# An encoder layer's output projection: where the squares for its RMS norm are added up, and on which engine

## The chip, the cores and the metric

The kernel runs on one core of a Trainium2 chip. The metric is the device time of one execution in microseconds (us); lower is better. Before the change the median of three runs is 1039.83 us, from 1038.88 to 1041.15.

## The reference

One encoder layer over 1024 tokens of width 1024. Two groups of attention heads (a sliding window and a two-dimensional neighbourhood) share one input projection; their outputs, each with an RMS norm of its own, go through one output projection. A gated MLP with a short convolution follows, and a last RMS norm:

```python
mix = jnp.concatenate([rmsnorm(o_a, norm_a[l]), rmsnorm(o_b, norm_b[l])], axis=-1)
h = h + jnp.einsum('bse,ed->bsd', mix, w_out[l])
hn = rmsnorm(h, norm_ffn[l])
h = h + conv_gated_mlp(hn, w_gate[l], w_up[l], conv_w[l], conv_b[l], w_down[l])
```

The norm divides each token by the root of the mean of its 1024 squares plus 1e-6. The change is in how `rmsnorm(h, norm_ffn[l])` gets its sums of squares, and in the first weights of the MLP.

## The kernel before, in words

Features lie on partitions: `h1[d]` (d = 0 to 7) holds 128 features of all 1024 tokens, and `at(d, h)` is its half h of 512 tokens. Products run in pairs of high and low float16 parts, three matmuls for one, accumulated in PSUM.

**The order of work.** TensorE's order is the order of the program text (`manual_schedule` for that engine). The order on the other engines is set by a planner, which takes what its estimates say is ready, by the order of the program, and earlier for what stands under `tc.high_priority(offset=...)`. Each engine then works strictly in the order that it was given, so an instruction that waits holds up all behind it on its engine.

**The output projection's second part** (group B's four input tiles) is the loop over half h and tile d. Each (h, d) is one product of twelve matmuls (L180, `product16`, which yields after each three), written to the PSUM banks `o`, `s` and `pj` in turn. `settle_out` follows it: VectorE adds the product onto `h1` (L1199), ScalarE's queue sends `h1` to DRAM (L1200), and ScalarE squares it into a tile `s2` (L1203). For d = 1, 2 and 3 VectorE adds the square onto the running total (L1205). From d = 3 on, the total and the four squares after it are addends, five a half: `sum_up` (L1216) sums each over its partitions with four matmuls whose moving operand is one column of `ones` (1/1024), into four columns of a PSUM bank, 128 tokens each. It does so two products later, so that TensorE need not wait. `inverse_root` adds EPS on VectorE (L1221) and raises to the power -0.5 on GpSimd (L1222). `widen` (L263) spreads the result over 128 partitions with four transposes, into the PSUM bank `sw`, and `normed` (L1227) multiplies `h1` by it. `operands` (L1183 on ScalarE, L1184 on VectorE) makes the float16 pairs `hg`: `B[1, 1]` from d = 0 to 3 and `B[2, 1]` from d = 4 to 7 of half 0.

**The MLP** uses a Strassen-like scheme of seven products a weight block, `p1` to `p7`, with sums of blocks of weights and of operands. The first four blocks (`HEAD`) are prepared inside the projection's loop: `settle_scales` finds scales, `pure` and `two_parts` (L1067, L1068) split weights, `head_weights` (L1237 for "s1", L1229 for later sums and differences) adds blocks of weights, and `split_w` (L1150, L1151) splits them. `units[0].p1()`, `units[1].p1()`, `units[0].p2()` and `units[1].p2()` follow the projection at once; the `p1` read `B[1, 1]` and the `p2` read `B[2, 1]`. Half 0's `widen` stands after product (1, 2), half 1's after `units[1].p2()`. Half 1's operands `B["t1"]` and on come from it.

**Buffers.** The squares and the four weight sums `wsum` share eight buffers of the tag `tt`; the weight sums keep four of them.

**A helper that is there already** (L221 to L225), and that the change calls. It sums over partitions by transposing into a bank and reducing:

```python
def inverse_power(sq, dim, tag):
    ps = bank("st", tag)
    for c in range(4):
        nc.tensor.transpose(ps[:, c * 128:(c + 1) * 128], sq[:, c * 128:(c + 1) * 128], ident)
    v = cpool.tile([128, 4], F32, name="v4", tag="v4", bufs=4)
    nc.vector.tensor_reduce(v, ps[:, :].rearrange("p (c w) -> p c w", w=128), axis=mybir.AxisListType.X, op=ALU.add)
    nc.vector.tensor_scalar(v, v, 1.0 / dim, EPS, op0=ALU.mult, op1=ALU.add)
    nc.gpsimd.tensor_tensor(v, v, minus_half, op=ALU.pow)
    return v
```

Of the kernel before, what the change touches and what calls it, by code (L numbers as in the profile page):

```python
# [13 lines left out]
F32 = mybir.dt.float32  # L14
# [4 lines left out]
ALU = mybir.AluOpType  # L19
PSUM = bass.MemoryType.PSUM  # L20

D, S, HD = 1024, 1024, 64
KT = D // 128
# [6 lines left out]
EPS = 1e-6  # L30
# [33 lines left out]
def hybrid_layer(tc, xT, w_in, w_out, w_gate, w_up, w_down, small, sink, rpb, consts, rope, out):  # L64
    nc = tc.nc
    with ExitStack() as ctx:
        pool = lambda name, bufs, **kw: ctx.enter_context(tc.tile_pool(name=name, bufs=bufs, **kw))
        cpool = pool("const", 1)
# [12 lines left out]
        def big(name, tag, dt=F32):  # L81
            return lpool.tile([128, S], dt, name=name, tag=tag, bufs=slots[tag])
# [9 lines left out]
        def bank(name, tag):  # L92
            return psum.tile([128, HALF], F32, name=name, tag=tag)
# [7 lines left out]
        ones = cpool.tile([128, 128], F32, name="ones")  # L101
# [5 lines left out]
        minus_half = cpool.tile([128, 4], F32, name="minus_half")  # L107
# [68 lines left out]
        def product16(ps, ws, xs, h):  # L176

            for i, (w, x) in enumerate(zip(ws, xs, strict=True)):
                for a, b in ((w[0], x[h][0]), (w[0], x[h][1]), (w[1], x[h][0])):
                    nc.tensor.matmul(ps, a, b, start=i == 0 and b is x[h][0] and a is w[0], stop=i == len(ws) - 1 and a is w[1])  # L180
                yield
# [35 lines left out]
# [10 lines that stand above are left out]
# [393 lines left out]
        mg, h1, norm = [None] * 8, [None] * KT, {}  # L620
# [106 lines left out]
        t = quarters(big("f", "mix"))  # L727
# [174 lines left out]
        for g in range(2):  # L902
            for b in range(NB):
                q, t, w = unit_window(g, b)
# [52 lines left out]
        for u in range(len(flat)):  # L957
            q, t, need, kind, _ = flat[u]
# [105 lines left out]
        def two_parts(view, src, by):  # L1064

            hi, lo = view
            nc.scalar.activation(hi, src, AF.Copy, scale=by)  # L1067
            nc.vector.scalar_tensor_tensor(lo, src, by, hi, op0=ALU.mult, op1=ALU.subtract)  # L1068
            return [(hi[:, j, :], lo[:, j, :]) for j in range(4)]

        def parts_places():

            t = big("wp", "op").bitcast(F16)[:, :].rearrange("p (d s k c) -> p d s k c", d=2, s=2, c=128)
            return [(t[:, i, 0], t[:, i, 1]) for i in range(2)]

        def pure(f):
            raw, by = head_raw[f][0], scale_of[f]
            to = parts_places()
            W[f, "11"], W[f, "12"] = two_parts(to[0], raw[:, 0:4], by), two_parts(to[1], raw[:, 4:8], by)
# [8 lines left out]
        def load_wo(d, pools):  # L1088
            raw = wo_raw.pop(d)
            if d % 2 == 0:  # L1090
                wo_raw["t"] = big("wo", "op").bitcast(F16)[:, :].rearrange("p (d s j c) -> p d s j c", d=2, s=2, c=128)
            t = wo_raw["t"][:, d % 2]
            with tc.high_priority(offset=300):
                nc.scalar.activation(t[:, 0], raw, AF.Copy, scale=wo_by)
                with behind(*["rows"] * (d >= 2)):
                    nc.vector.scalar_tensor_tensor(t[:, 1], raw, wo_by, t[:, 0], op0=ALU.mult, op1=ALU.subtract)
            return [(t[:, 0, j, :], t[:, 1, j, :]) for j in range(4)]
# [6 lines left out]
        with behind("flip", "xr"):  # L1104
            for d in range(0, WO_EARLY, 2):
                t = big("wr", "op")[:, :].rearrange("p (d j c) -> p d j c", d=2, c=128)
# [9 lines left out]
        for h in range(2):  # L1116
# [9 lines left out]
            if h == 0:  # L1126
                wo = [load_wo(d, wpool) for d in range(2)]
# [62 lines left out]

        K1, K2 = range(0, 4), range(4, 8)
        B = {}
        late, total, addends, narrow, ADDED = [], [None, None], [], [None, None], (4, 4)
        at = lambda k, h: h1[k][:, tsl(h)]

        def settle_out():
            d, h, ps = late.pop(0)
            with tc.high_priority(offset=300):
                nc.vector.scalar_tensor_tensor(at(d, h), ps, wo_back, at(d, h), op0=ALU.mult, op1=ALU.add)  # L1199
            nc.scalar.dma_start(spilled[d][:, tsl(h)], at(d, h))  # L1200
            s2 = half("s2")
            with tc.high_priority(offset=300):
                nc.scalar.activation(s2, at(d, h), AF.Square)  # L1203
                if 0 < d < ADDED[h]:
                    nc.vector.tensor_tensor(s2, s2, total[h], op=ALU.add)  # L1205
            total[h] = s2
            if d >= ADDED[h] - 1:
                addends.append((h, d, s2))

        def sum_up(until=2 * KT):  # L1210
            while addends and KT * addends[0][0] + addends[0][1] <= until:
                h, d, s2 = addends.pop(0)
                if d == ADDED[h] - 1:
                    narrow[h] = bank("ss", "pt")
                for c in range(4):
                    nc.tensor.matmul(narrow[h][:, c:c + 1], s2[:, c * 128:(c + 1) * 128], ones[:, 0:1], start=c == 0 and d == ADDED[h] - 1,  # L1216
                                     stop=d == KT - 1, skip_group_check=True)

        def inverse_root(h):
            v = cpool.tile([128, 4], F32, name="v4", tag="v4", bufs=4)  # L1220
            nc.vector.tensor_scalar(v, narrow[h][:, 0:4], EPS, None, op0=ALU.add)  # L1221
            nc.gpsimd.tensor_tensor(v, v, minus_half, op=ALU.pow)  # L1222
            return v

        def normed(h, wide, ds):
            for d in ds:
# [6 lines left out]
        def head_weights(i, name):  # L1233
            f, t = FO[i], wsum[i]
            g, u = head_raw[f]
            if name == "s1":
                nc.vector.tensor_tensor(t, u[:, 0:4], u[:, 4:8], op=ALU.add)  # L1237
            elif name == "s2":
                sub(t, t, g[:, 0:4])
            elif name == "s4":  # L1240
                sub(t, g[:, 4:8], t)
            elif name == "s3":
                sub(t, g[:, 0:4], u[:, 0:4])
            else:
                t = u[:, 4:8]
            if name == "s1":
                if i % 2 == 0:
                    s1_places.extend(parts_places())
                W[f, name] = two_parts(s1_places.pop(0), t, scale_of[f])
            else:  # L1250
                W[f, name] = split_w(t, 4, scale_of[f])
# [4 lines left out]
        for d in range(WO_EARLY, KT):  # L1256
            if d % 2 == 0:
                t = fpool.tile([128, KT, 128], F32, name="raw", tag="raw", bufs=3)
            wo_raw[d] = t[:, 4 * (d % 2):4 * (d % 2) + 4]
            nc.sync.dma_start(wo_raw[d], w_out[d, :, 4:8, :])  # L1260
        for h in range(2):
            for d in range(KT):
                if h == 0 and len(wo) < KT:
                    wo.append(load_wo(len(wo), fpool))
                ps = bank("pj", ("o", "s", "pj")[(h * KT + d) % 3])
                for _ in product16(ps, wo[d], mg[4:8], h):
                    pass
                late.append((d, h, ps))
                sum_up(KT * h + d - 2)
                if h == 1 and d == 1:  # L1270
                    with tc.high_priority(offset=300):
                        v = inverse_root(0)
                settle_out()
                if (h, d) in SETTLE_AT:
                    settle_scales(SETTLE_AT[h, d], 2, "pt")
                for f in PURE_AT.get((h, d), ()):
                    pure(FO[f])
                for when, name in ((S1_AT, "s1"), (S2_AT, "s2"), (S4_AT, "s4")):
                    for i, x in enumerate(when):
                        if x == (h, d):  # L1280
                            head_weights(i, name)
                if h == 1 and d == 2:
                    wide = widen(v, "pt")
                    normed(0, wide, K1)
                    B[1, 1] = operands([at(k, 0) for k in K1], "mix", "mix")
                if h == 1 and d == 4:
                    normed(0, wide, K2)
                    B[2, 1] = operands([at(k, 0) for k in K2], "mix", "mix")
# [174 lines left out]
        units = [Gated(f, ("o", "o", "pj", "pj")[i], ("s", "s", "pt", "pt")[i], "xg") for i, f in enumerate(FO[:HEAD])]  # L1463
        units[0].p1()
        units[1].p1()
        units[0].p2()
        with tc.high_priority(offset=300):
            sum_up()
            v = inverse_root(1)
        units[1].p2()  # L1470
        wide = widen(v, "pt")
        normed(1, wide, K1)
# [124 lines left out]
        for i, f in enumerate(FO[HEAD:]):  # L1597
            u = Gated(f)
# [135 lines left out]
        for i, (p, j, c) in enumerate(order):  # L1734
# [9 lines left out]
            ps = banks[p, j]  # L1744
# [31 lines left out]
        for k, cols in enumerate(quarters):  # L1776
            for j in (2, 3):
                ps = banks[6, j]
# [109 lines left out]
```

## Time and profile before

| what | value |
|---|---|
| median of three runs | 1039.83 us (1038.88 to 1041.15) |
| profiled execution, span from first to last instruction | 1035.9 us |
| profiled execution, its own total time | not given |
| TensorE busy, share of the span | 1011.7 us, 98% |
| VectorE busy | 880.0 us, 85% |
| ScalarE busy | 679.3 us, 66% |
| GpSimd busy | 214.1 us, 21% |
| granted TensorE clock, mean | 0.997 |

In the profile PE is TensorE's matmuls and PEld its weight loads, which overlap them; DVE is VectorE, ACT ScalarE, POOL GpSimd and SP the engine whose queue issues most transfers. L1205 is line 1205 of the kernel. In a list of instructions in order of time, a row has the start in us from the start of the span, the duration, engine, line, operation, tiles and shapes; neighbours of one kind are merged (x8 is eight of them) and an idle time before a row stands in brackets with what ended it. In a list of groups a row has the count, the busy time in us, the mean duration in ns, and the idle time before.

### The profile page before, as it was taken

How to read it: one execution, taken by the hardware profiler on the slowest of the kernel's cores; microseconds unless marked ns; L12 is line 12 of the kernel's file. 1: busy time of each engine (PE TensorE's matmuls, PEld its weight loads, DVE VectorE, ACT ScalarE, POOL GpSimd, SP SyncE). 2: the span in 40 equal slices, each digit the busy share in tenths (PEclk: the TensorE clock that was granted, in tenths of full speed). 3: DMA queues.
4: the chain of work that ended last, by engine and by line, in shares of the span. 5: the costliest groups of instructions: out<-in, count | busy, mean ns of one | idle time of the engine just before them, and what ended most of it. 6: DMA issues, size and time to landing. Idle time of an engine off the chain costs nothing.

```text
span 1035.9 us, 15696 instructions
## 1 busy us (share of the span) xinstructions
PE 1011.7 (98%) x5102; PEld 577.3 (56%) x5102; DVE 880.0 (85%) x1748; ACT 679.3 (66%) x1243; POOL 214.1 (21%) x341
## 2 busy tenths in 40 slices
PE   9998999999999999999999999999999999999996
PEld 7776777777775545544444444444444444444446
DVE  6699998766898699899898988888888879899875
ACT  8567787767687587645777777754535656655551
POOL 2235455676866301000000000000000000000002
PEclk9999999999999999999999999999999999999998
DMA  9447473676689775300687867733232778878744
GB/s 347 155 98 149 109 139 83 151 168 140 134 180 224 213 276 193 121 1 21 222 266 261 276 241 250 251 111 133 82 112 102 240 252 297 301 250 264 255 153 163
DMA packets 144275, 191.28 MB, mean 185 GB/s; under 512 B 77376, under 2 KB 88640, under 8 KB 144192
## 3 DMA queue, kind: packets, MB, share of 16 engines
q1 hardware_dynamic: 133536, 164.51, 54.7%
q10 hardware_dynamic: 10656, 25.76, 6.4%
q8 instruction: 40, 0.66, 0.2%
q14 instruction: 43, 0.35, 0.1%
HBM read 132.81 MB, written 28.57 MB: 156 GB/s over the span
## 4 chain that ended last, share of the span: by engine, by line
PE 71%; DVE 6%; ACT 1%; DMA 1%; issue 1%; POOL 0%; ACTq 0%; DVEq 0%; SPq 0%; POOLq 0%
PE dn L1177 6%; PE dn L1178 6%; PE dn L1176 6%; PE pj L180 6%; PE z L1176 5%; PE z L1177 5%; PE z L1178 5%; PE y L1176 4%; PE y L1177 4%; PE y L1178 4%; PE x L1176 4%; PE x L1177 4%; PE x L1178 3%; PE pj L172 2%; PE pj L174 2%; PE pj L173 2%
## 5 line engine op out<-in xcount | busy, mean ns | idle before, releaser
L1178 PEld LDWEIGHTS <-wlo 128*128 128x128 f16 x898 | 87.9, 98 | 101.3 <-DVE wlo L1151 0.2
L1176 PEld LDWEIGHTS <-whi 128*128 128x128 f16 x898 | 88.1, 98 | 100.3
L1177 PEld LDWEIGHTS <-whi 128*128 128x128 f16 x898 | 87.9, 98 | 100.3 <-issue 0.2
L1178 PE MATMUL dn<-xd,wlo 128*128 128x512 f16 (+1 forms) x330 | 120.4, 365 | 0.0
L1177 PE MATMUL dn<-xd,whi 128*128 128x512 f16 (+1 forms) x330 | 120.4, 365 | 0.0
L1176 PE MATMUL dn<-xd,whi 128*128 128x512 f16 (+1 forms) x330 | 120.4, 365 | 0.0
L172 PE MATMUL pj<-xgh,whi 128*128 128x512 f32 x248 | 106.8, 431 | 0.8 <-ACT whi L156 0.8
L1177 PE MATMUL z<-hg,whi 128*128 128x512 f16 x264 | 100.1, 379 | 0.0
L1178 PE MATMUL z<-hg,wlo 128*128 128x512 f16 x264 | 100.1, 379 | 0.0
L1176 PE MATMUL z<-hg,whi 128*128 128x512 f16 x264 | 100.1, 379 | 0.0
L466 ACT ACTIVATE p<-p,nm 128x385 f32<-128x385 f32 (+3 forms) x128 | 74.8, 585 | 38.0 <-DVE nm L462 33.3
L174 PE MATMUL pj<-xgh,wlo 128*128 128x512 f32 x248 | 97.9, 395 | 1.4 <-POOL wlo L157 1.4
L173 PE MATMUL pj<-xgl,whi 128*128 128x512 f32 x248 | 97.5, 393 | 0.0
L1150 ACT ACTIVATE whi<-ws,m 128x512 f16<-128x512 f32 (+1 forms) x96 | 65.9, 709 | 35.6 <-DVE ws L1317 19.5
L1151 DVE SCALAR_TENSOR_TENSOR wlo<-ws,m,whi 128x512 f16<-128x512 f32 (+1 forms) x96 | 70.2, 741 | 17.8 <-ACT whi L1150 17.6
L1031 POOL TENSOR_TENSOR back<-back,cst 128x4 f32<-128x4 f32 (+1 forms) x7 | 2.8, 396 | 356.7 <-DVE back L1030 356.7
L1165 ACT ACTIVATE scan<-scan 128x1024 f32<-128x1024 f32 (+1 forms) x60 | 61.1, 1019 | 17.0 <-DMA scan<-in_w_down_dram 12.3
L1150 ACT ACTIVATE whi<-raw,m 128x512 f16<-128x512 f32 (+1 forms) x78 | 51.4, 700 | 17.9 <-DMA raw<-in_w_down_dram 12.7
L1151 DVE SCALAR_TENSOR_TENSOR wlo<-raw,m,whi 128x512 f16<-128x512 f32 (+1 forms) x78 | 55.4, 732 | 7.5 <-ACT whi L1150 6.9
L1176 PE MATMUL y<-hg,whi 128*128 128x512 f16 x160 | 60.6, 379 | 0.0
L1177 PE MATMUL y<-hg,whi 128*128 128x512 f16 x160 | 60.6, 379 | 0.0
L1178 PE MATMUL y<-hg,wlo 128*128 128x512 f16 x160 | 60.6, 379 | 0.0
(291 smaller groups left out, 2465.5 us busy)
## 6 DMA issues: line engine op xcount, KB each, us to landing
xd<-x SPq DMA_DIRECT2D x77, 256.0 KB, 5.4
raw<-in_w_down_dram SPq DMA_DIRECT2D x64, 256.0 KB, 3.8
x<-c ACTq DMA_DIRECT2D x22, 512.0 KB, 3.5
scan<-in_w_gate_dram SPq DMA_DIRECT2D x18, 512.0 KB, 4.7
scan<-in_w_up_dram SPq DMA_DIRECT2D x18, 512.0 KB, 4.3
raw<-in_w_gate_dram SPq DMA_DIRECT2D x18, 512.0 KB, 3.8
raw<-in_w_up_dram SPq DMA_DIRECT2D x18, 512.0 KB, 4.4
raw<-in_w_in_dram SPq DMA_DIRECT2D x32, 256.0 KB, 3.1
```

The costliest lines, as they stand in the source:

```text
L172: nc.tensor.matmul(ps, w[0], x[0][:, tsl(h)], start=first, stop=False)
L173: nc.tensor.matmul(ps, w[0], x[1][:, tsl(h)], start=False, stop=False)
L174: nc.tensor.matmul(ps, w[1], x[0][:, tsl(h)], start=False, stop=last)
L180: nc.tensor.matmul(ps, a, b, start=i == 0 and b is x[h][0] and a is w[0], stop=i == len(ws) - 1 and a is w[1])
L466: nc.scalar.activation(p[:, 0:e], p[:, 0:e], AF.Exp, bias=nm, scale=-1.0, accum_out=sm)
L1031: nc.gpsimd.tensor_tensor(back, back, unit_back.to_broadcast([128, n]), op=ALU.mult)
L1150: mark["whi"] = nc.scalar.activation(hi, src, AF.Copy, scale=by)
L1151: nc.vector.scalar_tensor_tensor(lo, src, by, hi, op0=ALU.mult, op1=ALU.subtract)
L1165: nc.scalar.activation(t, t, AF.Square, accum_out=dst)
L1176: nc.tensor.matmul(ps, w[0], x[0], start=first and i == 0, stop=False, skip_group_check=True)
L1177: nc.tensor.matmul(ps, w[0], x[1], start=False, stop=False, skip_group_check=True)
L1178: nc.tensor.matmul(ps, w[1], x[0], start=False, stop=last and i == len(ws) - 1, skip_group_check=True)
```

## The change

All squares of a half are now added up to one tile: d = 1 to 6 on GpSimd, d = 7 on VectorE. This tile alone is transposed (`inverse_power`), in place of the five addends summed by the column of ones; `sum_up` and `inverse_root` go. Half 0's transposes stand in the middle of product (1, 1), half 1's between `units[1].p1()` and `units[0].p2()`; the two `widen` stay where they are. The four weight sums "s1" of the first blocks go from VectorE to GpSimd.

```diff
             with tc.high_priority(offset=300):
                 nc.scalar.activation(s2, at(d, h), AF.Square)
-                if 0 < d < ADDED[h]:
-                    nc.vector.tensor_tensor(s2, s2, total[h], op=ALU.add)
+                if d:
+                    (nc.vector if d == KT - 1 else nc.gpsimd).tensor_tensor(s2, s2, total[h], op=ALU.add)
             total[h] = s2
-            if d >= ADDED[h] - 1:
-                addends.append((h, d, s2))
-
-        def sum_up(until=2 * KT):
...
-        def inverse_root(h):
...
             if name == "s1":
-                nc.vector.tensor_tensor(t, u[:, 0:4], u[:, 4:8], op=ALU.add)
+                nc.gpsimd.tensor_tensor(t, u[:, 0:4], u[:, 4:8], op=ALU.add)
...
-                for _ in product16(ps, wo[d], mg[4:8], h):
-                    pass
+                for i, _ in enumerate(product16(ps, wo[d], mg[4:8], h)):
+                    if (h, d, i) == (1, 1, 1):
+                        with tc.high_priority(offset=300):
+                            v = inverse_power(total[0], D, "pt")
                 late.append((d, h, ps))
-                sum_up(KT * h + d - 2)
-                if h == 1 and d == 1:
-                    with tc.high_priority(offset=300):
-                        v = inverse_root(0)
                 settle_out()
...
         units[0].p1()
         units[1].p1()
+        with tc.high_priority(offset=300):
+            v = inverse_power(total[1], D, "pt")
         units[0].p2()
-        with tc.high_priority(offset=300):
-            sum_up()
-            v = inverse_root(1)
         units[1].p2()
         wide = widen(v, "pt")
         normed(1, wide, K1)
```

More of the change, by code (lines that the diff above doesn't have):

```diff
@@ L1192, in hybrid_layer @@
         B = {}
-        late, total, addends, narrow, ADDED = [], [None, None], [], [None, None], (4, 4)
+        late, total = [], [None, None]
         at = lambda k, h: h1[k][:, tsl(h)]
@@ L1203, in settle_out @@
                 nc.scalar.activation(s2, at(d, h), AF.Square)
-                if 0 < d < ADDED[h]:
-                    nc.vector.tensor_tensor(s2, s2, total[h], op=ALU.add)
+                if d:
+                    (nc.vector if d == KT - 1 else nc.gpsimd).tensor_tensor(s2, s2, total[h], op=ALU.add)
             total[h] = s2
-            if d >= ADDED[h] - 1:
-                addends.append((h, d, s2))
-        def sum_up(until=2 * KT):
[L1211 to L1217, printed above, removed]
-        def inverse_root(h):
[L1220 to L1223, printed above, removed]
         def normed(h, wide, ds):
```

## The prediction

> **What bounds the kernel now.** I read the page's busy shares first, then the busy time by stage, then TensorE's and VectorE's instructions in order of time around the change.
>
> ```profile
> PE 1011.7 (98%) x5102; PEld 577.3 (56%) x5102; DVE 880.0 (85%) x1748; ACT 679.3 (66%) x1243; POOL 214.1 (21%) x341
> ```
>
> ```profile
> 386.00:424.00 38.00, 38.00 (x214) 21.76 (x213) 35.88 (x58) 27.32 (x47) 3.07 (x4) 1.00 0.53 180
> 432.00:486.00 54.00, 54.00 (x253) 24.54 (x252) 53.76 (x80) 28.95 (x41) 0.00 (x0) 1.00 0.01 4
> ```
>
> The columns of the second fence are the stretch, its length, then the busy time of PE, PEld, DVE, ACT and POOL. TensorE never stops in either stretch (38.00 of 38.00, 54.00 of 54.00), at full granted clock (1.00). VectorE is busy for 35.88 of 38.00 us and then for 53.76 of 54.00. GpSimd does 3.07 us in the first. So TensorE sets the time, with VectorE barely 2 us behind, and both must become faster together.
>
> **TensorE's side.** The order of TensorE's work is written out by hand, so its gaps can be read off.
>
> ```profile
> 386.19 0.95 PE L1216 MATMUL ss<-ones,s 128*128 128x1 f32 x8
> 387.00 2.75 PE L180 MATMUL pj<-mg,wo 128*128 128x512 f16 x12
> ...
> 403.18 0.60 PE L263 MATMUL sw<-cst,v 128*128 128x128 f32 x4
> 403.62 7.93 PE L180 MATMUL pj<-mg,wo 128*128 128x512 f16 x36
> ...
> 424.17 0.38 PE L1176 MATMUL x<-hg,wp 128*128 128x512 f16 x1
> ...
> 426.75 1.84 PE L1216 MATMUL ss<-ones,s 128*128 128x1 f32 x16
> 428.46 0.38 PE L1176 MATMUL x<-hg,wp 128*128 128x512 f16 x1
> ```
>
> ```profile
> 358.07 0.87 PE st L221 x8
> ```
>
> One addend by the ones column holds TensorE for 387.00 - 386.19 = 0.81 us. Eight stand alone between products and two together (428.46 - 426.75 = 1.71 us): 8 x 0.81 + 1.71 = 8.2 us removed. Added are two sets of four transposes (L221, in the chain of waits two sets in 0.87 us; L263's four take 403.62 - 403.18 = 0.44): 2 x 0.44 = 0.9 us. Net 7.3 us, if TensorE finds its operands in time. The squares on ScalarE stay; no DMA is added or moved.
>
> **VectorE's side.** Three adds a half leave VectorE (d = 1, 2, 3), one a half comes (d = 7), four weight sums s1 leave, and each half gains a reduction of the transposed bank; the small addition of EPS is only replaced.
>
> ```profile
> 358.54 1.29 DVE L223 TENSOR_REDUCE v<-st 128x4 f32<-128x512 f32 x2
> ...
> 381.13 0.69 DVE L1205 TENSOR_TENSOR s<-s,s 128x512 f32<-128x512 f32 x1 [0.62 <-ACT s L1203]
> ...
> 388.91 1.27 DVE L1237 TENSOR_TENSOR ws<-rw 128x512 f32<-128x512 f32 x2
> ...
> 399.98 0.75 DVE L1199 SCALAR_TENSOR_TENSOR h<-pj,wo_back,h 128x512 f32<-128x512 f32 x1 [0.66 <-PE pj L180]
> ...
> 403.38 0.75 DVE L1199 SCALAR_TENSOR_TENSOR h<-pj,wo_back,h 128x512 f32<-128x512 f32 x1 [0.59 <-PE pj L180]
> ...
> 412.39 1.89 DVE L1184 TENSOR_TENSOR hg<-h,hg 128x512 f16<-128x512 f32 x3
> ...
> 414.98 0.75 DVE L1199 SCALAR_TENSOR_TENSOR h<-pj,wo_back,h 128x512 f32<-128x512 f32 x1 [0.71 <-PE pj L180]
> ...
> 421.69 2.53 DVE L1184 TENSOR_TENSOR hg<-h,hg 128x512 f16<-128x512 f32 x4
> ...
> 428.63 0.16 DVE L1221 TENSOR_SCALAR v<-ss 128x4 f32<-128x4 f32 x1 [2.54 <-PE ss L1216]
> ```
>
> Follow-on instructions overlap by a little: two L1237 take 1.27 us, so one takes about 0.60 of the queue, and a reduction 1.29 / 2, about 0.6. The tightest meeting is units[0].p2 at 424.17, which multiplies by B[2, 1]; VectorE makes that in the four L1184 from 421.69, so the first is ready near 422.35, with 1.8 us to spare. By then eight of the addends and both sets of transposes have passed, so TensorE would ask for it 8 x 0.81 - 0.9 = 5.6 us earlier, at 418.57. VectorE's queue up to there loses 10 x 0.6 = 6.0 us and gains three of 0.6 (two adds, one reduction; the second reduction falls behind this point): 4.2 us. It can also close its idle time up to there, 0.62 + 0.66 + 0.59 + 0.71 = 2.6 us. Without any other cost it is ready at 422.35 - 4.2 - 2.6 = 415.55, before TensorE asks. Afterwards VectorE has 2.54 us of idle time at 428.63 and the half-1 operands keep the same distance behind the widening, so the removal of the pair at 426.75 (1.71 us) is kept.
>
> **What the adds cost on GpSimd.** Sixteen additions of 128x512 arrive there: six a half and four s1. No row of before has GpSimd adding in this stage, so I bound it by the nearest rows.
>
> ```profile
> L328 DVE SCALAR_TENSOR_TENSOR kb<-t,cst,ka x16: 733/924/1744, 140.3 to 314.2; 128x512 fp32r<-128x512 f32 x16
> ```
>
> ```profile
> 196.99 1.30 POOL L157 TENSOR_TENSOR wlo<-raw,whi 128x512 fp32r<-128x512 f32 x1
> ...
> 197.09 1.74 DVE L328 SCALAR_TENSOR_TENSOR kb<-t,cst,ka 128x512 fp32r<-128x512 f32 x1
> ```
>
> ```profile
> 1010.56 4.03 DVE L1705 SCALAR_TENSOR_TENSOR h<-h,par,sw 128x512 f32<-128x512 f32 x6
> ...
> 1011.44 2.51 POOL L1703 TENSOR_TENSOR h<-h,wide 128x512 f32<-128x512 f32 x2 [173.45 <-ACT wide L1699]
> ```
>
> L328 reads two tensors from SBUF. Alone it takes 0.733 us; begun 0.10 us behind a GpSimd add of the same size it took 1.74, so it stood still for 1.01. L1705 reads one of its tensors (sw) from PSUM: six of them beside two GpSimd multiplications took 4.03 us, 0.67 each, with nothing lost. So an add on GpSimd takes 1.25 to 1.30 us of its own, and costs VectorE between 0 and 1.01 us, by what VectorE wants next. [...]
>
> ```profile
> L1199 DVE SCALAR_TENSOR_TENSOR h<-pj,wo_back,h 128x512 f32<-128x512 f32 x15 | 11.2, 747 | 2.1 <-PE pj L180 2.0
> L1068 DVE SCALAR_TENSOR_TENSOR wp<-rw,m,wp 128x512 f16<-128x512 f32 x8 | 5.8, 744 | 0.0
> L1227 DVE SCALAR_TENSOR_TENSOR h<-h,cst,sw 128x512 f32<-128x512 f32 x8 | 5.7, 743 | 0.0
> L1184 DVE TENSOR_TENSOR hg<-h,hg 128x512 f16<-128x512 f32 x8 | 5.1, 686 | 0.0
> ...
> L1151 DVE SCALAR_TENSOR_TENSOR wlo<-ws,m,whi 128x512 f16<-128x512 f32 x5 | 3.6, 744 | 0.0
> L1068 DVE SCALAR_TENSOR_TENSOR wp<-ws,m,wp 128x512 f16<-128x512 f32 x4 | 2.9, 748 | 0.0
> L1229 DVE TENSOR_TENSOR ws<-ws,rw 128x512 f32<-128x512 f32 x4 | 2.7, 684 | 0.0
> ```
>
> These are VectorE's large groups from 376 to 424 that stay. From two SBUF tensors: 5.8 + 5.1 + 3.6 + 2.9 + 2.7 = 20.1 us; with a PSUM input: 11.2 + 5.7 = 16.9. So 54% of the work can be stopped, and an add that falls anywhere costs 0.54 x 1.01 = 0.55 us. For the second half the place can be seen: a square ends, and GpSimd's add begins.
>
> ```profile
> 404.23 0.63 ACT L1203 ACTIVATE s<-h 128x512 f32<-128x512 f32 x1 [0.90 <-DVE h L1199]
> ...
> 407.66 0.62 ACT L1203 ACTIVATE s<-h 128x512 f32<-128x512 f32 x1
> ...
> 415.77 0.63 ACT L1203 ACTIVATE s<-h 128x512 f32<-128x512 f32 x1 [1.59 <-DVE h L1199]
> ```
>
> ```profile
> 405.31 0.74 DVE L1227 SCALAR_TENSOR_TENSOR h<-h,cst,sw 128x512 f32<-128x512 f32 x1
> ...
> 407.89 1.40 DVE L1227 SCALAR_TENSOR_TENSOR h<-h,cst,sw 128x512 f32<-128x512 f32 x2
> ...
> 416.85 1.40 DVE L1227 SCALAR_TENSOR_TENSOR h<-h,cst,sw 128x512 f32<-128x512 f32 x2
> ```
>
> The adds of (1, 2), (1, 3) and (1, 6) would meet L1227, which reads sw from PSUM: no loss. That of (1, 5) would meet the three L1184 from 412.39: the full 1.01. The other twelve I take at 0.55: 6.6. Sum 7.6 us, of ends at 0 and 16 x 1.01 = 16.2; I take 7.6 since it is counted from the neighbours, and it assumes that the order of VectorE's work stays much as it is.
>
> **The sum.** VectorE is ready for units[0].p2 at 415.55 + 7.6 = 423.15, TensorE at 418.57. VectorE decides: 1.0 us earlier than 424.17, and 1.7 behind it, so 2.7 us of the 7.3 remain. The other price is a wait: the first half's transposes stand half-way in product (1, 1), and behind them on TensorE's queue stands everything. They need the add of d = 7, on VectorE, behind six adds in a chain on GpSimd; these need 6 x 1.30 = 7.8 us, and the s1 sums up to 5.2 more, in the six products from d = 1 to d = 7, 7.93 / 3 = 2.6 us each (the 36 matmuls at 403.62 are three): 15.9 us. That fits, and a TensorE stall there of up to 423.15 - 418.57 = 4.6 us would hide under VectorE's lateness, so I cost it at nothing; without that cover it costs its length. ScalarE's copy of a summed weight (L1067) now waits for GpSimd; other squares queue behind it; nothing by the same cover. The second half's transposes come 2.6 us after an add that VectorE has made: nothing.
>
> All of this is against the profiled execution (span 1035.9 us). Its own total time isn't given; the median of the three runs, 1039.83, lies 3.9 us above the span, for what lies around it, and I subtract from the median: 1039.83 - 2.7 = 1037.1.
>
> **The rivals.** With L for what the port takes from VectorE, the change of time is L - 10.3 us (1.0 + 1.7 + 7.6), and never below -7.3.
>
> *All of it is gained.* L is at most 3.0, 0.19 us an add, because the planner puts the adds beside L1199 and L1227 or because VectorE's order changes in favour of B[2, 1]. For it: the three free meetings above. Against it: 54% of the work can be stopped. 1039.83 - 7.3 = 1032.5. Chance 0.17.
>
> *Part of it*, my forecast: 1037.1, with a range of its own of 1034 to 1039 (L from 4.5 to 9.5). Chance 0.38.
>
> *No change.* L near 10.3, 0.65 an add: the saving on TensorE is eaten, 1039.8. It also comes out if GpSimd's chain is late at d = 7 and VectorE, which works in order, stands behind its last add as it stood 0.62 us for a square at 381.13. Chance 0.22.
>
> *Slower: the shared port makes VectorE the bound.* Place: the L1184 that make B[2, 1], before units[0].p2. From 0.78 us an add (L = 12.4) it is slower by more than 0.2%; at 1.01 on all sixteen, 16.2 - 10.3 = 5.9 us, 1045.7. For it: VectorE has 2.6 us of idle time to give, and twelve L1068 and eight L1184 lie on its way, all of which can be stopped. Against it: the PSUM-fed L1199 precedes each square and often follows. Chance 0.23. [...]
>
> **How the numbers follow.** About 0.2% (2.1 us) is what a measurement of this kernel can tell from no change. Faster by more: all of the first case and 0.28 of the second, 0.45. Within: 0.10 of the second and the third, 0.32. Slower: 0.23. The range runs from just under the full gain, 1032.3, to 1042.5, into the slower case until about 0.12 of it and 0.05 below are left out.
>
> **What would show it.** L1216 gone, eight L221 more, TensorE's out projection without its 0.81 us gaps. Sixteen GpSimd additions of about 1.3 us between 372 and 420, some stretched. L1184, L1068, L1151 and L1229 with means above 744 and 684 ns, the excess near 7.6 us; L1199 and L1227 unchanged. TensorE waiting at units[0].p2 for hg L1184, and perhaps at the transposes in (1, 1). It is wrong if the two-input groups keep their means and no wait for hg appears (1032.5), or if TensorE waits for VectorE for more than 7 us there.

## The result and the profile after

The changed kernel takes 1046.82 us in the median of six runs (1043.73 to 1049.42), the kernel before 1039.36 in six runs beside it: a ratio of 1.0074, 95% interval 1.0062 to 1.0087. It is 7.5 us slower, where a gain and 1037.1 were predicted, in a range that ended at 1042.5. What came out is the slower rival, with VectorE as the bound, at another place than the one it named: TensorE waits at the transposes and not at units[0].p2. Taken once more on another chip, the changed kernel stood at 1.0073 (1.0046 to 1.0101). "The port", in the prediction and in what was expected of the runs, is the author's name for what lets a GpSimd addition stop a VectorE instruction. No row shows a port; the rows show the stops, 0.94 to 1.15 us for a full one.

The page's busy shares after, and the stages (length, then busy time of PE, PEld, DVE, ACT and POOL, granted clock, DMA share, GB/s):

```profile
PE 1007.9 (96%) x5030; PEld 568.9 (54%) x5030; DVE 889.5 (85%) x1742; ACT 678.2 (65%) x1243; POOL 237.0 (23%) x357
```

```profile
386.00:424.00 38.00, 29.18 (x131) 13.19 (x129) 37.38 (x49) 21.21 (x35) 18.60 (x15) 0.91 0.41 135
...
399.00:403.00 4.00, 0.00 (x0) 0.00 (x0) 4.00 (x6) 1.59 (x4) 1.63 (x1) 0.74 0.35 131
403.00:407.00 4.00, 2.73 (x9) 1.60 (x10) 4.00 (x7) 2.78 (x5) 0.00 (x0) 0.50 0.53 142
407.00:408.00 1.00, 1.00 (x5) 0.33 (x4) 0.38 (x3) 0.72 (x1) 0.59 (x1) 0.62 0.85 332
```

TensorE, which never stopped from 386 to 424 before, is now busy for 29.18 of these 38.00 us; VectorE went from 35.88 to 37.38, so it is full. The clock falls to 0.50 within the idle stretch (0.74 over 399 to 403) and stays there behind it until about 407.8 us (0.50 over 403 to 407, 0.62 over the next one). TensorE's instructions in order of time show where it stands:

```profile
393.79 1.89 PE L180 MATMUL pj<-mg,wo 128*128 128x512 f16 x8
404.27 1.08 PE L221 MATMUL st<-cst,s 128*128 128x128 f32 x4 [8.59 <-DVE s L1205]
405.15 5.35 PE L180 MATMUL pj<-mg,wo 128*128 128x512 f16 x18
410.33 0.60 PE L263 MATMUL sw<-cst,v 128*128 128x128 f32 x4
...
430.62 0.63 PE L221 MATMUL st<-cst,s 128*128 128x128 f32 x4 [1.56 <-DVE s L1205]
436.27 0.60 PE L263 MATMUL sw<-cst,v 128*128 128x128 f32 x4
```

There is no wait for hg at units[0].p2. TensorE stands 8.59 us at the first half's transposes in product (1, 1), for VectorE's add of d = 7, and 1.56 us at the second half's. VectorE's groups from 376 to 424, to be set beside the means before (744 to 748 for L1068 and L1151, 742 for L1096, 684 for the sums, now L1212, 686 for L1184, about 160 for L243 and L244):

```profile
L1199 DVE SCALAR_TENSOR_TENSOR h<-pj,wo_back,h 128x512 f32<-128x512 f32 x14 | 10.4, 741 | 0.6 <-PE pj L180 0.6
L1068 DVE SCALAR_TENSOR_TENSOR wp<-rw,m,wp 128x512 f16<-128x512 f32 x8 | 7.9, 1016 | 0.0
L1068 DVE SCALAR_TENSOR_TENSOR wp<-ws,m,wp 128x512 f16<-128x512 f32 x4 | 5.0, 1264 | 0.0
L1151 DVE SCALAR_TENSOR_TENSOR wlo<-ws,m,whi 128x512 f16<-128x512 f32 x5 | 4.6, 946 | 0.0
L1210 DVE SCALAR_TENSOR_TENSOR h<-h,cst,sw 128x512 f32<-128x512 f32 x6 | 4.2, 736 | 0.0
L1212 DVE TENSOR_TENSOR ws<-ws,rw 128x512 f32<-128x512 f32 x4 | 3.8, 950 | 0.0
L1096 DVE SCALAR_TENSOR_TENSOR wo<-raw,wo_by,wo 128x512 f16<-128x512 f32 x2 | 3.7, 1864 | 0.0
L1184 DVE TENSOR_TENSOR hg<-h,hg 128x512 f16<-128x512 f32 x4 | 3.0, 785 | 0.0
L243 DVE TENSOR_SCALAR m<-m 128x2 int32<-128x2 int32 x2 | 2.5, 1252 | 0.0
...
L244 DVE TENSOR_SCALAR m<-m 128x2 int32<-128x2 int32 x2 | 1.4, 692 | 0.0
```

The groups with a PSUM input (L1199, L1210) keep their 741 and 736 ns. All groups shown that read two SBUF tensors are stretched, and so are L243 and L244, which read one and take 0.16 us alone. Summed over every VectorE instruction of 370 to 440 us against its own shortest duration in the kernel before, the excess is 13.1 us: 9.8 on the first ten additions (six squares of half 0 and four s1, up to 401 us), 3.3 on the six of half 1. Of the 13.1 us, 3.3 lie on three L243 and L244. The lateness that this makes is seen in the last links ahead of the transposes, on VectorE, ScalarE and GpSimd:

```profile
401.46 0.74 DVE L1199 SCALAR_TENSOR_TENSOR h<-pj,wo_back,h 128x512 f32<-128x512 f32 x1
```

```profile
402.23 0.63 ACT L1203 ACTIVATE s<-h 128x512 f32<-128x512 f32 x1 [2.41 <-DVE h L1199]
```

```profile
403.44 0.68 DVE L1205 TENSOR_TENSOR s<-s,s 128x512 f32<-128x512 f32 x1
```

```profile
399.35 1.63 POOL L1205 TENSOR_TENSOR s<-s,s 128x512 f32<-128x512 f32 x1 [2.62 <-ACT s L1203]
```

Product (0, 7) ended 18 matmuls (of 0.216 us) ahead of 393.79 + 1.89 = 395.68, at 391.8. VectorE picks it up (L1199) only at 401.46, 9.7 us later; the square and the last add follow within 2 us. GpSimd's own chain was not late: ahead of d = 6 it had been idle for 2.62 us, waiting for a square that waited for VectorE.

### The profile page after: what moved, and what is told of

It reads as the page before. It is cut to its first block, busy times and chain, and to the rows that moved or that the text cites. A ratio compares the mean times of both kernels' runs of the same rounds, so it can differ in the third digit from the quotient of the medians.

```text
span 1044.5 us, 15579 instructions
## 1 busy us (share of the span) xinstructions
PE 1007.9 (96%) x5030; PEld 568.9 (54%) x5030; DVE 889.5 (85%) x1742; ACT 678.2 (65%) x1243; POOL 237.0 (23%) x357
## 4 chain that ended last, share of the span: by engine, by line
PE 60%; DVE 14%; DMA 2%; issue 2%; ACT 2%; SPq 0%; POOL 0%; ACTq 0%; DVEq 0%; POOLq 0%
PE z L1177 5%; PE z L1178 5%; PE z L1176 5%; PE dn L1178 4%; PE dn L1176 4%; PE dn L1177 4%; PE y L1178 4%; PE y L1177 4%; PE y L1176 4%; PE x L1176 3%; PE pj L180 3%; PE x L1178 3%; PE x L1177 3%; PE pj L172 2%; PE pj L174 2%
## 5 line engine op out<-in xcount | busy, mean ns | idle before, releaser
L1151 DVE SCALAR_TENSOR_TENSOR wlo<-ws,m,whi 128x512 f16<-128x512 f32 (+1 forms) x96 | 71.3, 753 | 17.5 <-ACT whi L1150 17.5
L1165 ACT ACTIVATE scan<-scan 128x1024 f32<-128x1024 f32 (+1 forms) x60 | 61.0, 1017 | 16.2 <-DMA scan<-in_w_down_dram 13.4
L1151 DVE SCALAR_TENSOR_TENSOR wlo<-raw,m,whi 128x512 f16<-128x512 f32 (+1 forms) x78 | 55.5, 733 | 7.1 <-ACT whi L1150 7.0
```

The costliest lines, as they stand in the source:

```text
L1165: nc.scalar.activation(t, t, AF.Square, accum_out=dst)
```

## The experiments

Each run's ratio is against the kernel before on the same chip; a gain or loss in us is the difference of the medians there, unless it is said to be by the ratio. "Excess" is the sum over VectorE's stretched instructions, as above.

**The changed kernel again.** No edit.

> The changed kernel once more, for a second profile beside these. If the 3.7 us that its first profile lost late in the w_down products (TensorE waiting for weights between 980 and 992 us) belong to the change, they come again there; if they are a matter of one execution's transfers, this profile is without them and the wait at the first transposes is again 8 to 9 us.

1044.90 us, ratio 1.0073 (1.0046 to 1.0101).

```profile
404.38 1.09 PE L221 MATMUL st<-cst,s 128*128 128x128 f32 x4 [8.59 <-DVE s L1205]
```

The wait repeats to the hundredth, the excess (13.1 us) to the tenth. The first profile of the changed kernel had lost another 3.7 us between 834 and 1010 us, waiting for weights of the down projection; this one lost nothing there against before. So that part belongs to single executions. At half 1's widening (436.27 us, 431.05 before) the two profiles are 5.2 and 5.1 us behind before; at 339 us they had been 0.3 and 0.2 ahead, so 5.5 and 5.3 us were lost between.

**GpSimd's additions taken away, everything else left.** Sums of squares and of weights are not computed here.

```diff
-                    (nc.vector if d == KT - 1 else nc.gpsimd).tensor_tensor(s2, s2, total[h], op=ALU.add)
+                    if d == KT - 1:
+                        nc.vector.tensor_tensor(s2, s2, total[h], op=ALU.add)
+                    else:
+                        nc.gpsimd.memset(s2, 1.0)
...
-                nc.gpsimd.tensor_tensor(t, u[:, 0:4], u[:, 4:8], op=ALU.add)
+                nc.gpsimd.memset(t, 1.0)
```

> The changed kernel with each of its sixteen GpSimd additions replaced by a GpSimd instruction that only writes the same tile (a constant), so the sums of squares and the s1 weight sums are left out; VectorE's two additions of d = 7, the transposes, and the order of every engine's work stay as in the changed kernel. The sets still wait for the squares but not for the addition before, and take about 0.53 us in place of 1.3. Theory of the port (VectorE's lateness comes from GpSimd's reads alone): VectorE's two-input groups at 744 and 684 ns, excess under 1 us, no wait of TensorE over 1 us at the first half's transposes, and what was predicted without the port: 7.3 us below before, about 1031 to 1033 us. Theory of the order (the changed order of ScalarE's and VectorE's work delays the operands, as it did with all adds on VectorE): TensorE still waits 4 us or more at the transposes, and the time is within 3 us of before or above it.

1033.53 us, ratio 0.9944 (0.9930 to 0.9957): 4.7 us below before by the medians (1038.21 there), 5.8 by the ratio. Stage, TensorE, then VectorE:

```profile
386.00:424.00 38.00, 38.00 (x183) 17.94 (x182) 38.00 (x63) 31.46 (x53) 8.68 (x15) 1.00 0.56 181
```

```profile
394.63 2.10 PE L180 MATMUL pj<-mg,wo 128*128 128x512 f16 x9
396.64 0.63 PE L221 MATMUL st<-cst,s 128*128 128x128 f32 x4
397.10 4.05 PE L180 MATMUL pj<-mg,wo 128*128 128x512 f16 x18
```

```profile
393.83 0.74 DVE L1199 SCALAR_TENSOR_TENSOR h<-pj,wo_back,h 128x512 f32<-128x512 f32 x1
...
395.81 0.68 DVE L1206 TENSOR_TENSOR s<-s,s 128x512 f32<-128x512 f32 x1
```

VectorE and ScalarE do the same instructions in the same order as in the changed kernel. With no addition by GpSimd, VectorE's excess is 0.4 us, the transposes run without a wait, and VectorE picks up product (0, 7) 1.0 us after its end (396.73 - 18 x 0.216 = 392.84) in place of 9.7. This profile is 1.3 us behind that of before at 339 us and 5.9 ahead of it at half 1's widening: 7.2 us gained between. Between this kernel and the changed one lie 4.7 + 7.5 = 12.2 us of time (5.8 + 7.5 = 13.3 by the ratio), and 12.7 us of VectorE's excess. The 0.4 us that are left lie on two instructions: an L243 and an L244 that met a set took 0.36 and 0.40 us in place of 0.16 and ended as the set ended. The sets also drop the additions' dependence on each other and are 0.8 us shorter; that GpSimd was idle ahead of d = 6 speaks against either being what mattered, and no run here takes them apart.

**GpSimd instructions that only write.** Before, with twelve sets of a spare tile behind the squares of d = 1 to 6.

```diff
+        spare = fpool.tile([128, S], F32, name="junk", tag="junk", bufs=1)[:, 0:HALF]
...
+                if 0 < d < KT - 1:
+                    nc.scalar.copy(spare[:, 0:1], s2[:, 0:1])
+                    nc.gpsimd.memset(spare, 0.0)
```

> The kernel before, with twelve GpSimd instructions that only write (a spare half tile set to zero, read by nobody), one behind each square of d = 1 to 6, in the places where the idle additions stood; a tiny ScalarE write of one column into that tile, 12 x about 0.2 us, holds each to its place. Theory that GpSimd must read SBUF through the shared port to stop VectorE: the two-input groups of VectorE keep 744 and 684 ns, an excess under 1 us in all, and the time is within 0.1% of before. Theory that any GpSimd instruction that touches SBUF stops it: an excess near the 5.6 us of the idle additions and about 1040.5 us (+2.6).

1039.09 us, ratio 1.0005 (0.9996 to 1.0014). GpSimd's group, then VectorE's:

```profile
L1209 POOL MEMSET junk<- 128x512 f32 x12 | 6.3, 525 | 33.3 <-ACT junk L1208 33.2
```

```profile
L1068 DVE SCALAR_TENSOR_TENSOR wp<-rw,m,wp 128x512 f16<-128x512 f32 x8 | 5.8, 742 | 0.0
```

Here the sets stop nothing: one from 387.17 to 387.70 us ran beside two L1096 that kept their 1.40 us for both, and the groups with two SBUF inputs keep their means (742 and 748 for L1068, 743 for L1151, 682 for L1184). So a GpSimd set, which reads nothing, does not stop a VectorE instruction with two SBUF inputs, and an addition, which reads SBUF, does. For the tiny L243 and L244 that does not follow: none of these twelve sets met one, and in the run above a set held them too.

**GpSimd additions that nobody needs.** Before, with twelve additions into the spare tile in the same places.

```diff
+        spare = fpool.tile([128, S], F32, name="junk", tag="junk", bufs=1)[:, 0:HALF]
...
+                if 0 < d < KT - 1:
+                    nc.gpsimd.tensor_tensor(spare, s2, s2, op=ALU.add)
```

> The kernel before, with twelve GpSimd additions (d = 1 to 6 of each half, each reading the square twice and writing a spare tile that nothing reads) added behind the squares. TensorE's and VectorE's own work is that of before. Theory P: VectorE loses 6 x 0.98 + 6 x 0.55 = 9.2 us, has about 4.4 us to give, and TensorE waits for about 4 to 5 us: 1043 to 1045, with the means of the two-input groups up and those of L1199 unchanged. Theory C (the chain of adds and the early place of the transposes make the wait, the port does not matter): no change, 1039.4 within 1 us.

1040.58 us, ratio 1.0026 (1.0014 to 1.0039). TensorE, then the clock:

```profile
390.92 1.05 PE L1219 MATMUL ss<-ones,s 128*128 128x1 f32 x8 [1.31 <-ACT s L1204]
391.84 4.44 PE L180 MATMUL pj<-mg,wo 128*128 128x512 f16 x12
```

```profile
392.00:396.00 4.00, 4.00 (x12) 1.50 (x11) 4.00 (x5) 4.00 (x7) 3.84 (x5) 0.57 0.88 338
```

Excess 5.5 us, with no result that anything waits for, and VectorE's and ScalarE's order as before: the kernel loses 0.26% from interference alone. Both are less than expected (9.2 us, and a wait of 4 to 5 us); an addition here reads one tile twice and takes 1.04 us where nothing holds it. TensorE waits only 1.31 us, for a square whose input VectorE made late; the next twelve matmuls then take 4.44 us in place of 2.75, at a clock of 0.57. That is 1.7 us more.

**Squares alone, or sums alone.** The changed kernel with the s1 sums back on VectorE; and before with only those sums on GpSimd (the same line the other way round).

```diff
-                nc.gpsimd.tensor_tensor(t, u[:, 0:4], u[:, 4:8], op=ALU.add)
+                nc.vector.tensor_tensor(t, u[:, 0:4], u[:, 4:8], op=ALU.add)
```

> The changed kernel with the four s1 sums back on VectorE; the squares' adds stay on GpSimd. Theory P (the shared port: each GpSimd add stops VectorE, about 0.98 us each in the first half, and the late VectorE makes the square of d = 7 late, for which TensorE's transposes wait): four stops (3.9 us) go, four sums of 0.6 us come back, VectorE is 1.5 us less late; TensorE's wait at the first transposes falls from 8.6 to about 7 us, time about 1045. Theory Q (GpSimd's own queue: 5.6 us of sums stand between the adds and make the chain late): the wait falls by up to 5.6 us, to 3 us or less, time about 1041.

1039.66 us, ratio 1.0017 (1.0007 to 1.0028).

```profile
400.40 1.09 PE L221 MATMUL st<-cst,s 128*128 128x128 f32 x4 [3.91 <-DVE s L1205]
```

> The kernel before with only the four s1 sums moved to GpSimd. Theory P (the shared port): four stops of VectorE, about 1 us each in this part, less 2.4 us of work taken off: VectorE 1.6 us later, which the kernel before has to give (2.6 us of idle time, 1.8 us at units[0].p2): within 0.6 us of the kernel before. Theory S (ScalarE's copies of the summed weights wait for GpSimd and hold up the squares behind them): TensorE waits at the sums of the ones column, 2 us or more slower.

1040.45 us, ratio 1.0026 (1.0013 to 1.0039).

```profile
389.58 2.33 PE L180 MATMUL pj<-mg,wo 128*128 128x512 f16 x10 [1.69 <-DVE wo L1096]
```

```profile
384.00 1.26 DVE L243 TENSOR_SCALAR m<-m 128x2 int32<-128x2 int32 x1
...
385.78 1.25 DVE L244 TENSOR_SCALAR m<-m 128x2 int32<-128x2 int32 x1
386.94 1.86 DVE L1068 SCALAR_TENSOR_TENSOR wp<-rw,m,wp 128x512 f16<-128x512 f32 x1
388.72 0.15 DVE L245 TENSOR_SCALAR m<-m 128x2 f32<-128x2 f32 x1
388.79 1.40 DVE L1096 SCALAR_TENSOR_TENSOR wo<-raw,wo_by,wo 128x512 f16<-128x512 f32 x2
```

With the squares alone VectorE loses 8.2 us to twelve additions (0.68 each), and the wait at the transposes is less than half. Neither theory had its size: P expected 7 us of waiting and Q at most 3. The wait fell by 4.7 us and VectorE's excess by 4.9, which fits P's cause; against Q's stands that GpSimd was idle ahead of d = 6 in the changed kernel. The sums were expected to be nearly free; they lose 3.6 us to four (0.90 each), of which 2.2 on two instructions of 128x2, and VectorE then reaches the split of wo[6] (L1096) too late for product (0, 6). The clock stayed at 1.00 after that wait of 1.69 us. The two kernels lie 1.9 and 2.5 us above before, 4.4 together, and the change as a whole 7.5: the parts draw on the same cover. In both runs the planner also changed the order of VectorE's and ScalarE's work, so their sizes are not the stops' alone.

**One half alone.** The squares of half 0, or of half 1, on GpSimd and transposed; the other half and the sums as before. GP holds the half: (0,) or (1,).

```diff
-                if 0 < d < ADDED[h]:
+                if h in GP:
+                    if d:
+                        (nc.vector if d == KT - 1 else nc.gpsimd).tensor_tensor(s2, s2, total[h], op=ALU.add)
+                elif 0 < d < ADDED[h]:
                     nc.vector.tensor_tensor(s2, s2, total[h], op=ALU.add)
...
+        if 1 in GP:
+            with tc.high_priority(offset=300):
+                v = inverse_power(total[1], D, "pt")
```

> The first half's squares alone on GpSimd with one transposed addend; the second half and the s1 sums as before. TensorE saves 5 x 0.81 - 0.44 = 3.6 us. Theory P with the place of the loss in the first half: TensorE waits for about 4 us at the transposes and runs at a lower clock for some us after it; with squares of both halves 1.8 us slower and the second half alone 2.7 us faster, this should be 2 to 4.5 us slower than the kernel before. If the loss were spread over both halves: faster or the same.

1040.48 us, ratio 1.0024 (1.0013 to 1.0036).

```profile
399.54 1.09 PE L221 MATMUL st<-cst,s 128*128 128x128 f32 x4 [3.91 <-DVE s L1207]
```

> The second half's squares alone on GpSimd with one transposed addend; the first half and the s1 sums as before. TensorE saves 3 x 0.81 + 1.71 - 0.44 = 3.7 us. Theory P: there the adds cost VectorE about 0.55 us each, 3.3 us, less than it has to give (4.4 us, and 1.2 us of adds taken from it), so all is gained: about 1035.7. Theory C: the second half's transposes come too early for a chain of adds as well (1.6 us of waiting in the changed kernel): 1037.3. If the adds cost 0.98 us here too, about 1038.

1035.11 us, ratio 0.9975 (0.9964 to 0.9986). And once more on another chip:

> The second half's squares alone on GpSimd, as in the run named for the second half, taken once more beside its neighbour below. If the gain there was real: ratio 0.9975 within 0.001, so about 1035.2 us, no wait of TensorE at the second half's transposes, and VectorE losing about 2 us to six additions (0.31 each). If it was the luck of one chip: a ratio of 1.000.

1034.66 us, ratio 0.9970 (0.9959 to 0.9982). TensorE in the second of the two runs, and VectorE's groups:

```profile
420.89 0.60 PE L221 MATMUL st<-cst,s 128*128 128x128 f32 x4
426.51 0.60 PE L263 MATMUL sw<-cst,v 128*128 128x128 f32 x4
```

```profile
L1184 DVE TENSOR_TENSOR hg<-h,hg 128x512 f16<-128x512 f32 x8 | 6.9, 910 | 0.0
L1068 DVE SCALAR_TENSOR_TENSOR wp<-rw,m,wp 128x512 f16<-128x512 f32 x8 | 5.8, 744 | 0.0
```

Here only two L1184 are stopped, an excess of 1.9 us for six additions (0.31 each), and no wait arises at the transposes. This is the version that beats both kernels, by 2.7 and 3.9 us in the two runs. The first half, with the same number of additions, loses 4.7 us of VectorE (0.78 each) and shows the wait.

**All additions on VectorE.** The changed kernel with no addition on GpSimd.

```diff
-                    (nc.vector if d == KT - 1 else nc.gpsimd).tensor_tensor(s2, s2, total[h], op=ALU.add)
+                    nc.vector.tensor_tensor(s2, s2, total[h], op=ALU.add)
...
-                nc.gpsimd.tensor_tensor(t, u[:, 0:4], u[:, 4:8], op=ALU.add)
+                nc.vector.tensor_tensor(t, u[:, 0:4], u[:, 4:8], op=ALU.add)
```

> The changed kernel with all adds and the s1 sums on VectorE, one transposed addend a half: GpSimd adds nothing. VectorE has eight adds and one reduction more than before by units[0].p2, 5.4 us, and 2.6 us of idle time to close. Theory P: its operations keep their durations (L1068 0.745 us, L1096 0.742), TensorE waits 1 to 3 us, time about 1038.7 (1037 to 1040). Theory C: a chain with 0.7 us a step is early enough, no wait, the full 7.3 us: 1032.

1038.69 us, ratio 1.0006 (0.9996 to 1.0015). TensorE, then ScalarE:

```profile
400.92 1.08 PE L221 MATMUL st<-cst,s 128*128 128x128 f32 x4 [5.73 <-DVE s L1205]
```

```profile
393.66 1.06 ACT L1165 ACTIVATE scan<-scan 128x1024 f32<-128x1024 f32 x1 [0.49 <-DVE h L1199]
...
394.71 1.65 ACT L1203 ACTIVATE s<-h 128x512 f32<-128x512 f32 x3
```

No GpSimd addition, no excess, and yet 5.73 us of wait, more than the 1 to 3 expected: in this order the planner had put the squares of d = 5, 6 and 7 together, behind the scales' reads (L1165), on ScalarE. That is a second cause which gives the same symptom, and it is why the run with sets, which keeps the changed kernel's order, was needed to tell them apart.

**Second half on GpSimd, two more squares added on VectorE in the first.** Tried as an improvement.

```diff
-        late, total, addends, narrow, ADDED = [], [None, None], [], [None, None], (4, 4)
+        late, total, addends, narrow, ADDED = [], [None, None], [], [None, None], (6, 4)
+        GP = (1,)
```

> The second half as in the run above; in the first half VectorE adds two more squares (d = 4 and 5), so that three addends go through the ones column and not five. Theory of the port (VectorE's order was fine until GpSimd stopped it): TensorE saves 2 x 0.81 = 1.6 us more, VectorE pays 2 x 0.6 = 1.2 us with no stop, and the time is 1.6 us below the run above, about 1033.5. Theory of the order (any more links in the chain of adds in the first half make it end too late, as with all adds on VectorE): TensorE waits 1 to 3 us at the ones-column sums of d = 5 or 6, and the time is that of the run above or up to 2 us more.

1046.21 us, ratio 1.0081 (1.0067 to 1.0095).

```profile
398.75 1.84 PE L1220 MATMUL ss<-ones,s 128*128 128x1 f32 x8 [7.09 <-DVE s L1209]
```

```profile
395.07 1.65 ACT L1204 ACTIVATE s<-h 128x512 f32<-128x512 f32 x3
```

The theory of the order came out, far beyond the size given to it: again three squares together at 395.07, and a wait of 7.09 us. Two additions more on VectorE turn 0.9970 into 1.0081, with no GpSimd addition before that wait.

**The transposes later.** The changed kernel with the first half's transposes in product (1, 4), the widening behind (1, 5).

```diff
-                    if (h, d, i) == (1, 1, 1):
+                    if (h, d, i) == (1, 4, 1):
...
-                if h == 1 and d == 2:
+                if h == 1 and d == 5:
...
-                if h == 1 and d == 4:
+                if h == 1 and d == 6:
```

> The changed kernel with the first half's transposes three products later (in (1, 4)), its widening after (1, 5) and B[2, 1] after (1, 6). Theory P by VectorE's throughput: VectorE loses about as much to GpSimd (13 us), and the wait moves to the hg that units[0].p1 and p2 need: still 2 to 4 us slower than the kernel before. Theory C (the place of the transposes makes the wait, and the clock's fall behind it): the wait of 8.6 us and the low clock go, 1 us or less of waiting, and the time is 2 to 4 us below the kernel before.

1046.31 us, ratio 1.0082 (1.0064 to 1.0100). TensorE, then VectorE:

```profile
406.28 0.63 PE L221 MATMUL st<-cst,s 128*128 128x128 f32 x4 [0.83 <-DVE s L1205]
420.38 1.12 PE L263 MATMUL sw<-cst,v 128*128 128x128 f32 x4 [9.59 <-POOL v L225]
```

```profile
417.05 0.68 DVE L223 TENSOR_REDUCE v<-st 128x4 f32<-128x512 f32 x1
```

The wait moves to the widening and does not shrink: the reduction runs 10.8 us behind its transposes on VectorE's queue, which is never idle between (excess 13.5 us). The loss, 8.4 us, is twice the most that was expected. So the place of the transposes alone is not the cause. How much of the 10.8 us is lateness, and how much the place that the planner gave the reduction, this run does not tell.

## Why the prediction was wrong, point by point

**What TensorE saves** was right. It was put at 7.3 us; without GpSimd's additions the kernel gains 7.2 up to half 1's widening, and 5.8 (4.5 to 7.3) over the whole by the ratio, 4.7 by the medians.

**What VectorE can do without other cost** was right: with sets in place of additions, no operand of units[0].p2 is late.

**The price of GpSimd's additions** (the prediction's L, "what the port takes from VectorE"; no run shows a port, the runs show these stops) is the term that was mis-sized: 7.6 us taken, 13.1 measured. The price of one stop was right (the full stops are 0.94 to 1.15 us, against 1.01 taken), and the second half's six were near (2.1 taken, 3.3 measured). What failed is the mean over the stage. The share of 54% was taken over all of 376 to 424; but ten of the sixteen additions fall before 401 us, and there VectorE's work is, beside 6.7 us of L1199, mostly L1068 and L1096 (11.6 us before), all from two SBUF tensors. L1096 was not in the count, nor were L243 and L244, which are stopped too (1.23 to 1.27 us in place of 0.16). Nor is the chance of a hit the share of stoppable time: an instruction that passes in 0.74 us is followed by another while GpSimd's addition still runs, and the first that can be stopped is stopped. GpSimd's addition from 381.69 to 382.96 us let an L1199 and an L1011 (from PSUM) pass and held the L1068 behind them for 0.19 us; of the first ten stretched instructions this is the only one held for less than 0.9. So the first ten additions cost 0.98 us each. The prediction took two SBUF inputs as the mark of what can be stopped, and that is not the whole of it: L243, with one input, took 1.25 us beside an addition and 0.36 beside a set, while no set held an instruction with two SBUF inputs. What makes L243 and L244 stop is not shown.

**"The other price is a wait ... I cost it at nothing"** is the step that failed in kind. By the prediction's own sum the measured price gives 13.1 - 10.3 = 2.8 us slower; 5.5 came between 339 us and half 1's widening. The cover assumed that TensorE's wait at the transposes is the same lateness as at units[0].p2, paid only once. But VectorE's loss lies ahead of the transposes (9.8 of 13.1 us), and the last links there, L1199, the square and the add of d = 7, all stand in or behind VectorE's queue. The test of whether GpSimd's 7.8 and 5.2 us fit in 15.9 looked at the queue that was not late. Measured: 8.59 + 1.56 us at the two transposes and 0.16 at wo[6]; some 1.75 us of low clock behind the long wait (the 18 matmuls 5.35 against 4.05 in the run with sets, the transposes 1.08 against 0.63); less 7.3. That is 4.8 of the 5.5; the other 0.7 is not placed. The second half's wait had been put at nothing as well. That the slower rival's 1045.7 lies near the measured 1046.82 is luck: it took more for the stops (16.2 us) and nothing for these waits and the clock.

**The clock** was not in the sum, nor was wo[6] as a tight meeting; the sums-only run shows that one at 1.69 us.

**Still open:** the medians say 7.5 and 7.0 us, the profiles 5.5 and 5.3 between 339 us and half 1's widening. Part of the rest arose late, between 834 and 1010 us, in one of the changed kernel's two profiles (3.7 us, and 5.0 in that of the kernel with sets); the changed kernel's runs scatter over 5.7 us, those of before over 2.9, and no run here tells why.

## What to carry to other kernels

Before work goes to GpSimd, count what VectorE does in the very microseconds in which it will run there, the tiny instructions too, and take one full stop an addition where most of it reads two SBUF tensors (0.98 us each for the first ten here); a mean over the stage was low by nearly half. Then follow the lateness along the in-order queue to the first instruction that TensorE waits for, which may be long before the operand that looked tightest. The same offload gained 2.7 to 3.9 us in the second half, where half of VectorE's large work reads PSUM (10.2 us of L1199 and L1227 from 401 to 424 us before), so offload by place, not by kind.

## What was not expected of the hardware

- Instructions of 128x2 that take 0.16 us (L243, L244, L245) are stopped by a GpSimd addition as long as large ones: up to 1.1 us more each (L243 1.27 and L244 1.23 in the changed kernel, L245 1.00 in the run with additions that nobody needs). L243 and L244 were also held by a set, which only writes (0.36 and 0.40 us), while no large instruction was.
- Around the 8.59 us in which TensorE stood the clock fell to 0.50, until about 407.8 us. After only 1.31 us ahead of ones-column sums it fell too (0.57 over 392 to 396; by the us 0.65, 0.50, 0.50 and 0.65, and 1.00 on both sides), but not after 1.69 us in the sums-only run:

```profile
392.00:396.00 4.00, 4.00 (x28) 2.67 (x28) 4.00 (x8) 3.68 (x7) 1.52 (x3) 1.00 0.48 157
```

That so short a wait can be followed by a fall of the clock is shown here; what decides it is not.
